# A hybrid encoder layer on one core: the raw sums of the FFN weights formed in the mixer, and seven products in every down projection

## The chip, the core and the metric

The kernel runs on one core of a Trainium2 chip. The time is what the device takes from the first to the last instruction of one execution and what lies around it, in microseconds (us); the figure given is the median of several runs. The engines: TensorE (PE; its weight loads are PEld in the profile), VectorE (DVE), ScalarE (ACT), GpSimd (POOL) and SyncE (SP), which here issues every DMA. Each engine runs its own instructions strictly in the order of the program and waits for others by semaphores.

## The reference, cut to what matters

2048 frames of a new stream and 64 frames of a running one (2112 tokens of 1024 features) pass through one layer in float32:

```
h = rmsnorm(x);  proj = h @ w_in
x = x + concat(gated_delta(proj), multiscale_pool(proj)) @ w_out
h = rmsnorm(x)
x = x + (silu(h @ w_gate) * (h @ w_up)) @ w_down      # 1024 -> 2816 -> 1024
y = rmsnorm(x)
```

The first addition is the mixer, the second the FFN. The change touches how the weights `w_gate`, `w_up` and `w_down` are prepared, and how the product with `w_down` is formed for a third of the tokens.

## The kernel before, in words

A float32 number is held as two float32r parts, hi and lo (a copy rounded by ACT, and by DVE what is left); each product of two such numbers is three matmuls: hi*hi, hi*lo, lo*hi. Making the two parts is called a split below: one cast on ACT and one subtraction on DVE.

The mixer runs over four blocks of 512 tokens (the first with the 64 more). Each block projects 21 column tiles (`pp`), runs the chunked delta rule of four heads (an inverse by doubling: the masked factors `Um` come from POOL, the products `py` and `pt` from PE, then `TV` from DVE; `NOUT` and `NX` say how many such chunks may be ahead of the one in use), pools, and projects out (`pz`) to `x2d` in DRAM.

The FFN runs over three blocks of 704 tokens. `gate_up` handles one of the 22 tiles f of 128 hidden features. It forms gate and up for both halves of the tokens (352 each) with seven products for the eight quarter products (Strassen's scheme): the weight factors are the quarters 11, 12, 22 and the sums S1 to S4 of quarters, the token factors 11, 21, 22 and T1 to T4. A product is 12 matmuls of 352 columns into one of the PSUM tiles x, y, z (`px`, `py`, `pz` in the profile); x is read by DVE twice on the way (tiles g and u) before the last product goes on into it.

The weights for this come from `prep_strassen`. The first time, in FFN block 0, it loads four raw quarters of a tile f, forms S1 to S4 on POOL (tiles `wrS`), splits all seven factors (`ws`, `wsS`) and stores the split S1 to S4 to DRAM (`gsd`). In blocks 1 and 2 it loads those four back in split form and splits only 11, 12 and 22.

The down projection runs over groups of 4, 4, 2, 4, 4, 4 tiles f. In block 0 it is dense: `down` takes eight column tiles m and both token halves, three matmuls for each f (PSUM tile d), adds into `y` on DVE, with the hidden features split by gate_up itself into `h3t`. In blocks 1 and 2 (`SDOWN`) it uses seven products: `factors` forms from each pair of tiles f the seven token factors (`hq` and `h7`; four sums on POOL, seven splits), `prep_down` forms for each pair of column tiles the raw sums on POOL (`wrda`, `wrdb`) from two loaded tiles (`wrdt`, `wrdl`) and splits seven factors (`wsd`, `wsdS`), and `down_strassen` adds the products dx, dy, dz into `y` in seven additions. The last group of block 2 is dense in both.

The order on every engine is set by `Machine`: it records all instructions, gives each a cost and a rank (its place in the program, moved by boosts for urgent ones), and lists them engine by engine as a list scheduler does. A `Chain` is a generator whose steps are mixed into the main program as its clock of PE work goes on; a step's rank comes from where it is mixed in, but the scheduler may place an instruction earlier when its engine is free and its operands are there.

The lines that the change meets:

```
SDOWN = (1, 2)
NY, NLEV, NOUT, NX = 3, 3, 5, 3
```

Of the kernel before, what the change touches and what calls it, by code (L numbers as in the profile page):

```python
# [11 lines left out]
F32 = mybir.dt.float32  # L12
F32R = mybir.dt.float32r
AF = mybir.ActivationFunctionType
ALU = mybir.AluOpType
# [3 lines left out]
P = 128  # L19
# [27 lines left out]

SDOWN = (1, 2)
# [305 lines left out]
def hybrid_kernel(ctx, tc, a, o):  # L354
# [88 lines left out]
    gsd = {nm: dpool.tile([NF, P, 1024], F32, tag=f"g{nm}", name=f"g{nm}") for nm in KEEP}  # L443
    hpd = dpool.tile([NB2, 7, 4, P, N2], F32, tag="hpd", name="hpd")
# [50 lines left out]
    def halves(b, gi):  # L495

        return ((0,), (1,)) if (b, gi) == (NB2 - 1, len(groups) - 1) else ((0, 1),)

    def plain(b, gi):
        return b not in SDOWN or len(halves(b, gi)) > 1  # L500

# [71 lines left out]
    def prep_strassen(key):  # L573
# [33 lines left out]
    def prep_down(m, f0, G):  # L607
# [654 lines left out]

    def new_o(B, pool=None, tag="op", bufs=2):
        four = [(pool or opool).tile([P, 4, 2, MB], F32R, tag=tag or f"h{k}", name=f"op{k}_{B.j}", bufs=bufs) for k in range(2)]
        B.o, B.o4 = [four[k // 4][:, k % 4] for k in range(KT)], four[0]
# [70 lines left out]
    for j in range(NBLK):  # L1336
# [13 lines left out]
        for h in range(NH):  # L1350
# [126 lines left out]
    def gate_up(b, f):  # L1477
# [44 lines left out]
        return raw if b in SDOWN else h3t[f % 6]  # L1522
# [54 lines left out]
    six = [opool.tile([P, 3, 2, TB2], F32R, tag="op", name=f"h3_{i}", bufs=2) for i in range(2)]  # L1577
    h3t = [six[i // 3][:, i % 3] for i in range(6)]
# [10 lines left out]
    for op in order:  # L1589
        b = op[1]  # L1590
        if op[0] == "gu":
# [6 lines left out]
            if b in SDOWN:  # L1598
                gi = max(g for g, (f0, G) in enumerate(groups) if f0 <= f)
                if plain(b, gi):  # L1600
                    if f == groups[gi][0] or f == groups[gi][0] + 2:
                        two = opool.tile([P, 2, 2, TB2], F32R, tag="op", name=f"h3l{f}", bufs=2)
                    for i in range(2):
                        split(two[:, f % 2], slice(i * N2, (i + 1) * N2), h3[f][:, i])
                    h3[f] = two[:, f % 2]
                elif f % 2:
                    h3[f] = factors(b, f, h3.pop(f - 1), h3[f])
# [29 lines left out]
NY, NLEV, NOUT, NX = 3, 3, 5, 3  # L1637
# [16 lines left out]
WAIT_STAT = 8.46  # L1654

# [110 lines left out]
```

## Time and profile before

| | us |
|---|---|
| median of 3 runs | 2418.33 (2416.62 to 2418.92) |
| span of the profiled execution | 2413.8 |
| PE busy | 2363.0 (98%) |
| DVE busy | 1744.6 (72%) |
| ACT busy | 1276.2 (53%) |
| POOL busy | 970.7 (40%) |
| DMA | 471.39 MB, mean 195 GB/s |

The profile is of one execution, whose span is given; the page states no separate time for that execution, so its own time is its span and the few us that lie around it. A row of a group gives the count, the busy time of the group, the mean duration of one instruction, and the idle time before them with what ended it. PE's matmuls overlap, so the mean of one (322 ns for 352 columns) is more than its share of the time; busy time over count is the share. In rows by stage, each stage begins with its limits and length, then the busy time of each engine with its instructions in brackets; the last three figures are PE's granted clock, the busy share of the DMA engines and GB/s. With a tile's name the same rows count that tile's instructions alone, and engines without any are left out.

### The profile page before, as it was taken

The page shows a single profiled execution, that of the slowest core. Times are in us where ns is not written, and L with a number is a line of the kernel's source. Part 1 is how long each engine was busy: PE and PEld are TensorE (multiplying, and loading weights), DVE is VectorE, ACT ScalarE, POOL GpSimd, SP SyncE. Part 2 cuts the span into 40 slices and gives each one's busy share as a digit, 9 for nine tenths or more (in the row PEclk, how much of TensorE's full clock was granted, in tenths as well). Part 3 has the DMA queues.
Part 4 walks back from the last instruction along what each step waited for, and adds up shares of the span by engine and source line. Part 5 has one row for each costly group of instructions (what it writes and reads, how often), then busy time and mean ns, then how long its engine had stood idle before and what let it go on. Part 6 is the DMA issues. An engine that isn't in the chain of part 4 may idle for free.

```text
span 2413.8 us, 42035 instructions
## 1 busy us (share of the span) xinstructions
PE 2363.0 (98%) x14811; PEld 2190.4 (91%) x14811; DVE 1744.6 (72%) x3065; ACT 1276.2 (53%) x2849; POOL 970.7 (40%) x1130
## 2 busy tenths in 40 slices
PE   8999999999999999999999999999999999999998
PEld 7889798778787878899999999999999999999998
DVE  7998774675467786787676765778777778777676
ACT  6665654563456464573454555554444564545444
POOL 1646442454246752365232235454222564223121
PEclk9999999999999999999999999999999999999999
DMA  7644566355555564987554557766644586454653
GB/s 266 222 156 151 174 221 217 134 181 175 179 182 182 186 196 138 317 298 238 200 183 166 184 199 237 238 227 204 224 157 147 163 292 216 144 168 166 202 171 109
DMA packets 219107, 471.39 MB, mean 195 GB/s; under 512 B 27408, under 2 KB 85776, under 8 KB 218896
## 3 DMA queue, kind: packets, MB, share of 16 engines
q1 hardware_dynamic: 218896, 468.71, 57.9%
q8 instruction: 116, 1.90, 0.3%
q14 instruction: 95, 0.78, 0.1%
HBM read 354.81 MB, written 113.80 MB: 194 GB/s over the span
## 4 chain that ended last, share of the span: by engine, by line
PE 80%; DVE 10%; DMA 4%; ACT 3%; issue 3%; POOL 1%; SPq 0%; DVEq 0%; POOLq 0%; ACTq 0%
PE pp L278 16%; PE px L278 16%; PE pz L278 11%; PE d L278 8%; PE py L278 7%; PE dx L278 5%; PE dy L278 3%; PE pk_p L278 2%; DVE hq L278 2%; PE pt_p L278 2%; PE dz L278 1%; ACT hr L278 1%; DVE hr L278 1%; PE px_p L278 1%; PE gr_p L278 1%
## 5 line engine op out<-in xcount | busy, mean ns | idle before, releaser
L278 PE MATMUL pp<-h,wsp 128*128 128x512 f32 (+1 forms) x2480 | 560.0, 367 | 3.9 <-DVE wsp L278 2.6
L278 PEld LDWEIGHTS pp<-h,wsp 128*128 128x128 f32 x2480 | 402.4, 191 | 53.7 <-ACT wsp L278 3.4
L278 POOL TENSOR_TENSOR Um_p<-Gst_p,lmask 128x256 f16<-128x256 f32 x224 | 169.9, 772 | 121.1 <-PE py_p L278 97.1
L278 PE MATMUL pz<-op,wsp 128*128 128x512 f32 (+1 forms) x960 | 215.7, 366 | 2.9 <-ACT op L278 2.6
L278 ACT CAST ws<-wr 128x512 fp32r<-128x512 f32 x198 | 121.9, 617 | 177.3 <-PE dx L278 46.9
L278 DVE TENSOR_TENSOR ws<-wr,ws 128x512 fp32r<-128x512 f32 x198 | 164.6, 835 | 45.9 <-ACT ws L278 40.9
L278 PEld LDWEIGHTS pz<-op,wsp 128*128 128x128 f32 x960 | 155.8, 190 | 23.0 <-ACT op L278 3.2
L278 PE MATMUL d<-h,wsd 128*128 128x352 f32 x1056 | 169.6, 322 | 0.5 <-ACT h L278 0.5
L278 PEld LDWEIGHTS d<-h,wsd 128*128 128x128 f32 x1056 | 168.5, 188 | 0.8 <-ACT h L278 0.8
L278 DVE TENSOR_TENSOR TV_p<-TV_p,pt_p 128x512 f16<-128x512 f16 x192 | 129.2, 681 | 43.1 <-PE pt_p L278 38.6
L278 PE MATMUL px<-hBT,ws 128*128 128x352 f32 x792 | 141.3, 326 | 12.7 <-DVE u L278 12.5
L278 POOL TENSOR_TENSOR wrS<-wr,wrS 128x512 f32<-128x512 f32 x44 | 63.9, 1452 | 209.2 <-DMA wrS<-in_wu_dram 97.3
L278 ACT ACTIVATE hr<-g 128x352 f32<-128x352 f32 x132 | 65.7, 498 | 153.7 <-DVE g L278 152.7
L278 PEld LDWEIGHTS px<-hBT,ws 128*128 128x128 f32 x792 | 127.9, 188 | 19.3 <-DVE u L278 18.5
L278 PE MATMUL px<-hA,ws 128*128 128x352 f32 x792 | 141.9, 322 | 0.1
L278 PE MATMUL px<-hA,wsS 128*128 128x352 f32 x792 | 138.6, 323 | 3.3 <-ACT g L278 3.2
L278 PE MATMUL pz<-hB,ws 128*128 128x352 f32 x792 | 141.5, 322 | 0.0
L278 PE MATMUL py<-hB,wsS 128*128 128x352 f32 x792 | 140.4, 322 | 0.0
L278 PE MATMUL px<-hBT,wsS 128*128 128x352 f32 x792 | 137.8, 322 | 1.3 <-ACT g L278 1.3
L278 PE MATMUL py<-hA,wsS 128*128 128x352 f32 x792 | 138.5, 323 | 0.1
L278 POOL TENSOR_TENSOR q<-hr,hr 128x352 f32<-128x352 f32 x40 | 45.0, 1126 | 231.5 <-DVE hr L278 230.1
L278 PEld LDWEIGHTS px<-hA,wsS 128*128 128x128 f32 x792 | 128.4, 188 | 5.4 <-ACT g L278 5.2
(613 smaller groups left out, 5737.4 us busy)
## 6 DMA issues: line engine op xcount, KB each, us to landing
wsS<-gS SPq DMA_DIRECT2D x176, 512.0 KB, 4.5
wsp<-wnd SPq DMA_DIRECT2D x126, 512.0 KB, 3.3
gS<-wsS SPq DMA_DIRECT2D x88, 512.0 KB, 4.4
wr<-in_wg_dram SPq DMA_DIRECT2D x132, 256.0 KB, 3.0
wnd<-wsp SPq DMA_DIRECT2D x42, 512.0 KB, 5.0
xd<-x2d SPq DMA_DIRECT2D x96, 176.0 KB, 3.2
wr<-in_wu_dram SPq DMA_DIRECT2D x66, 256.0 KB, 3.6
wrd<-in_wd_dram SPq DMA_DIRECT2D x56, 256.0 KB, 3.5
```

The source lines that it names most:

```text
L278: getattr(getattr(self.nc, op.eng), name)(*args, **kw)
```

## The change

A chain `weight_sums` is added and started when the first head of the mixer's second block is taken up. For each of the 22 tiles f it loads the four raw quarters, forms S1 to S4 on POOL in place (tiles gs0 to gs3, one buffer each) and stores them unsplit to DRAM (`grd`, named rS1 to rS4 in the rows). Then, for each group and each pair of column tiles of `w_down`, it loads two tiles, forms the four sums in place (ds0, ds1) and stores them to `drd`.

`prep_strassen` in FFN block 0 loads all seven raw factors, four of them from `grd`, and forms none. `prep_down` loads its two tiles of sums from `drd`. `SDOWN` goes: block 0 uses `factors`, `prep_down` and `down_strassen` as the others do, and `h3t` with the splits in gate_up goes. `NOUT` falls from 5 to 3 and `NX` from 3 to 2, which frees the space for the four buffers.

```diff
-SDOWN = (1, 2)
...
+    grd = {nm: dpool.tile([NF, P, 512], F32, tag=f"r{nm}", name=f"r{nm}") for nm in KEEP}
+    drd = dpool.tile([KT // 2, len(FGROUPS), 2, P, 512], F32, tag="drd", name="drd")
...
     def plain(b, gi):
-        return b not in SDOWN or len(halves(b, gi)) > 1
+        return len(halves(b, gi)) > 1
...
-        for nm, src in (("11", "11"), ("S1", "21"), ("22", "22"), ("12", "12")):
-            get(nm, src)
-        for nm in ("S3", "S2", "S4"):
-            raw[nm] = wtiles(nm, True)[0]()
-        gt = nc.gpsimd.tensor_tensor
-        gt(out=raw["S3"], in0=raw["11"], in1=raw["S1"], op=ALU.subtract)
-        gt(out=raw["S1"], in0=raw["S1"], in1=raw["22"], op=ALU.add)
-        gt(out=raw["S2"], in0=raw["S1"], in1=raw["11"], op=ALU.subtract)
-        gt(out=raw["S4"], in0=raw["12"], in1=raw["S2"], op=ALU.subtract)
+        for i, nm in enumerate(FW):
+            raw[nm] = wtiles(nm, i % 2 == 1)[0]()
+            nc.sync.dma_start(out=raw[nm], in_=grd[nm][key[1]] if nm in grd else q[nm])
...
-        gt = nc.gpsimd.tensor_tensor
-        left, right = slice(0, n), slice(n, 2 * n)
-        gt(out=s31[:, left], in0=top[:, left], in1=low[:, left], op=ALU.subtract)
-        gt(out=s31[:, right], in0=low[:, left], in1=low[:, right], op=ALU.add)
-        gt(out=s24[:, left], in0=s31[:, right], in1=top[:, left], op=ALU.subtract)
-        gt(out=s24[:, right], in0=top[:, right], in1=s24[:, left], op=ALU.subtract)
+        gi = [f for f, _ in groups].index(f0)
+        for i, x in enumerate((s31, s24)):
+            nc.sync.dma_start(out=x[:, : 2 * n], in_=drd[m, gi, i, :, : 2 * n])
+        right = slice(n, 2 * n)
...
+    def weight_sums():
+        gt = nc.gpsimd.tensor_tensor
+        new = lambda i, nm: gp.tile([P, 512], F32, tag=f"s{i}", name=nm, bufs=1)
+        for f in range(NF):
+            q = [new(i, f"gs{i}_{f}") for i in range(4)]
+            a11, a21, a22, a12 = q
+            for t, (nm, i) in zip(q, (("wg", 0), ("wu", 0), ("wu", 1), ("wg", 1))):
+                nc.sync.dma_start(out=t, in_=a[nm][f][:, i * 512 : (i + 1) * 512])
+            yield LAT_SUM
+            gt(out=a22, in0=a21, in1=a22, op=ALU.add)
+            gt(out=a21, in0=a11, in1=a21, op=ALU.subtract)
+            yield LAT_SUM
+            gt(out=a11, in0=a22, in1=a11, op=ALU.subtract)
+            gt(out=a12, in0=a12, in1=a11, op=ALU.subtract)
+            for nm, t in (("S1", a22), ("S3", a21), ("S2", a11), ("S4", a12)):
+                nc.sync.dma_start(out=grd[nm][f], in_=t)
+            yield LAT_SUM
+        at = 0
+        for gi, (f0, G) in enumerate(groups):
+            n = G // 2 * P
+            left, right = slice(0, n), slice(n, 2 * n)
+            for m in range(KT // 2):
+                top, low = (new(at + i, f"ds{i}_{gi}_{m}") for i in range(2))
+                at = 2 - at
+                for t, mm_ in ((top, m), (low, m + KT // 2)):
+                    nc.sync.dma_start(out=t[:, : 2 * n], in_=a["wd"][mm_][:, f0 * P : (f0 + G) * P])
+                yield LAT_SUM / 2
+                gt(out=low[:, right], in0=low[:, left], in1=low[:, right], op=ALU.add)
...
+                for i, t in enumerate((low, top)):
+                    nc.sync.dma_start(out=drd[m, gi, i, :, : 2 * n], in_=t[:, : 2 * n])
+                yield LAT_SUM / 2
...
+            if h == 0 and j == 1:
+                Chain(weight_sums())
...
-            if b not in SDOWN:
-                split(h3t[f % 6], slice(i * N2, (i + 1) * N2), e)
...
-NY, NLEV, NOUT, NX = 3, 3, 5, 3
+NY, NLEV, NOUT, NX = 3, 3, 3, 2
...
+LAT_SUM = 4.5
```

Three places in the order of the instructions. First POOL in the first block of the mixer, ahead of its first inverse (chist, ext and EL are small copies); before:

```order
L278 COPY chist_145<-ext0_4_170 128x3
L278 COPY ext0_9_232<-chist_145 128x3
L278 COPY ext0_9_232<-consts_93 128x3
L278 COPY chist_145<-ext0_8_177 128x3
L278 COPY EL_p0_0_0_215<-TV32_p0_0_0_213 128x2
```

and now:

```order
L276 TENSOR_TENSOR gs2_0_917<-gs1_0_916,gs2_0_917 128x512
L276 TENSOR_TENSOR gs1_0_916<-gs0_0_915,gs1_0_916 128x512
L276 COPY chist_150<-ext0_8_182 128x3
L276 COPY ext0_9_237<-chist_150 128x3
L276 COPY ext0_9_237<-consts_98 128x3
L276 TENSOR_TENSOR gs0_0_915<-gs2_0_917,gs0_0_915 128x512
L276 TENSOR_TENSOR gs3_0_918<-gs3_0_918,gs0_0_915 128x512
L276 COPY EL_p0_0_0_220<-TV32_p0_0_0_218 128x2
```

The sums of the first tile f stand in POOL's order from its row 25 on, a block earlier than the chain is started in the program; the last sum is its row 662 of 1099, shortly before the inverses of the fourth block. The sums of nine tiles f are ahead of the end of the second block's first inverse.

Next POOL in the second block of the mixer, within the inverse of head 1 (Um3 to Um6 are its masked factors); before:

```order
L278 TENSOR_TENSOR Um3_p1_1_0_1122<-Gst_p1_1_0_1045,lmask_140 128x256
L278 COPY EL_p1_1_1_1091<-TV32_p1_1_1_1089 128x2
L278 TENSOR_TENSOR Um4_p1_1_0_1137<-Gst_p1_1_0_1045,lmask_140 128x256
L278 TENSOR_TENSOR Gst_p1_1_1_1095<-Gam_p1_1_1_1094,consts_93 128x256
L278 TENSOR_TENSOR Um0_p1_1_1_1129<-Gst_p1_1_1_1095,lmask_140 128x256
```

and now:

```order
L276 TENSOR_TENSOR Um3_p1_1_0_1139<-Gst_p1_1_0_1062,lmask_145 128x256
L276 COPY ext1_3_1321<-chist_150 128x3
L276 TENSOR_TENSOR gs2_10_1363<-gs1_10_1362,gs2_10_1363 128x512
L276 TENSOR_TENSOR Um4_p1_1_0_1155<-Gst_p1_1_0_1062,lmask_145 128x256
L276 TENSOR_TENSOR gs1_10_1362<-gs0_10_1361,gs1_10_1362 128x512
L276 TENSOR_TENSOR Um5_p1_1_0_1170<-Gst_p1_1_0_1062,lmask_145 128x256
L276 TENSOR_TENSOR gs0_10_1361<-gs2_10_1363,gs0_10_1361 128x512
L276 TENSOR_TENSOR gs3_10_1364<-gs3_10_1364,gs0_10_1361 128x512
```

A sum now stands between any two Um of this inverse, and an Um behind it can start only when it is done.

Last SP, where the raw weights of FFN block 0's fourth tile f (number 120 in the names) are loaded; before:

```order
L278 DMA wr11_120_3034<-in_wg_dram 128x512
L278 DMA wrS1_120_3035<-in_wu_dram 128x512
L278 DMA y3_0_3115<-x2d_81 128x704
L278 DMA gS1_86<-wsS1_119_3028 128x1024
L278 DMA wr22_120_3036<-in_wu_dram 128x512
```

and now:

```order
L276 DMA wrS1_120_3176<-rS1_90 128x512
L276 DMA gS3_88<-wsS3_118_3158 128x1024
L276 DMA wr12_120_3178<-in_wg_dram 128x512
L276 DMA gS1_86<-wsS1_119_3169 128x1024
L276 DMA wr11_120_3175<-in_wg_dram 128x512
L276 DMA wrS4_120_3180<-rS4_93 128x512
L276 DMA wrS2_120_3177<-rS2_91 128x512
L276 DMA gS4_89<-wsS4_119_3173 128x1024
L276 DMA wrS3_120_3179<-rS3_92 128x512
```

Seven raw loads a tile f stand where four stood, between the same stores of split sums. SP's order has 1449 DMAs before and 1923 now.

More of the change, by code (lines that the diff above doesn't have):

```diff
@@ L1261, in fold_pool @@
                 yield LAT_APPLY
+    def weight_sums():
[26 more added lines that the diff above has]
+                gt(out=low[:, right], in0=low[:, left], in1=low[:, right], op=ALU.add)
+                gt(out=low[:, left], in0=top[:, left], in1=low[:, left], op=ALU.subtract)
+                gt(out=top[:, left], in0=low[:, right], in1=top[:, left], op=ALU.subtract)
+                gt(out=top[:, right], in0=top[:, right], in1=top[:, left], op=ALU.subtract)
+                for i, t in enumerate((low, top)):
+                    nc.sync.dma_start(out=drd[m, gi, i, :, : 2 * n], in_=t[:, : 2 * n])
+                yield LAT_SUM / 2
     def new_o(B, pool=None, tag="op", bufs=2):
@@ L1521, in gate_up @@
         finish(0, g1, x)
-        return raw if b in SDOWN else h3t[f % 6]
+        return raw
     def down(b, gi, h3, ys, which, done):
@@ L1576, in hybrid_kernel @@
     fpos = {2: (0, 1), 4: (0, 2, 1, 3)}
-    six = [opool.tile([P, 3, 2, TB2], F32R, tag="op", name=f"h3_{i}", bufs=2) for i in range(2)]
-    h3t = [six[i // 3][:, i % 3] for i in range(6)]
     h3, ys = {}, {}
@@ L1597, in hybrid_kernel @@
             h3[f] = gate_up(b, f)
[L1598 to L1607, printed above, removed]
+            gi = max(g for g, (f0, G) in enumerate(groups) if f0 <= f)
+            if plain(b, gi):
+                if f == groups[gi][0] or f == groups[gi][0] + 2:
+                    two = opool.tile([P, 2, 2, TB2], F32R, tag="op", name=f"h3l{f}", bufs=2)
+                for i in range(2):
+                    split(two[:, f % 2], slice(i * N2, (i + 1) * N2), h3[f][:, i])
+                h3[f] = two[:, f % 2]
+            elif f % 2:
+                h3[f] = factors(b, f, h3.pop(f - 1), h3[f])
             if f == NF - 1 and b + 1 < NB2:
```

## The prediction

> **What bounds the kernel now.** I read the page first, then the time by stage, then the waits in the two kinds of FFN block, last the instructions behind one wait. From the page: the span, the busy times and the chain that ended last.
>
> ```profile
> span 2413.8 us, 42035 instructions
> PE 2363.0 (98%) x14811; PEld 2190.4 (91%) x14811; DVE 1744.6 (72%) x3065; ACT 1276.2 (53%) x2849; POOL 970.7 (40%) x1130
> PE 80%; DVE 10%; DMA 4%; ACT 3%; issue 3%; POOL 1%; SPq 0%; DVEq 0%; POOLq 0%; ACTq 0%
> ```
>
> TensorE (PE) is the bound, so only removed matmuls or removed waits of PE can gain. The stages are cut by first and last start of a tile's matmuls (us, after the three durations): gate_up begins at 1003.2, block 0's dense down projection ends at 1474.3; the mixer I cut at 250, 480 and 700, block 1 at 1939.
>
> ```profile
> L278 PE MATMUL px<-hA,ws x792: 317/322/430, 1003.2 to 2359.6; 128*128 128x352 f32 x198
> ```
>
> ```profile
> L278 PE MATMUL d<-h,wsd x1056: 317/322/428, 1090.1 to 1474.1; 128*128 128x352 f32 x176
> ```
>
> ```profile
> core 0: us, PE busy (x) PEld busy (x) DVE busy (x) ACT busy (x) POOL busy (x), PEclk, DMA share, GB/s
> 0.00:250.00 250.00, 235.09 (x1785) 214.59 (x1786) 211.18 (x459) 159.19 (x399) 113.16 (x177) 0.99 0.60 202
> 250.00:480.00 230.00, 229.82 (x1529) 196.66 (x1529) 154.14 (x292) 124.45 (x310) 94.37 (x140) 1.00 0.54 182
> 480.00:700.00 220.00, 219.44 (x1302) 178.41 (x1301) 135.46 (x250) 110.51 (x278) 93.01 (x138) 1.00 0.51 173
> ...
> 1003.20:1474.30 471.10, 466.79 (x2910) 464.64 (x2909) 336.21 (x509) 241.64 (x488) 184.99 (x142) 1.00 0.63 219
> 1474.30:1939.00 464.70, 454.88 (x2783) 445.21 (x2783) 349.24 (x593) 238.57 (x494) 191.89 (x200) 1.00 0.60 199
> 1939.00:2366.00 427.00, 419.76 (x2575) 412.01 (x2574) 302.16 (x523) 212.66 (x440) 132.11 (x143) 1.00 0.58 191
> ```
>
> The clock is granted in full, so it plays no part. What one matmul of 352 columns costs comes from the dense down projection of block 0, by the tile wsd (columns PE, PEld, DVE, ACT; the first row is block 0, the second block 1).
>
> ```profile
> 1003.20:1474.30 471.10, 169.44 (x1056) 168.49 (x1056) 35.88 (x48) 27.79 (x48) 1.00 0.63 219
> 1474.30:1939.00 464.70, 76.62 (x391) 64.40 (x390) 37.10 (x48) 22.91 (x48) 1.00 0.60 199
> ```
>
> 169.44/1056 = 0.1605 us. By it block 0's 2910 matmuls need 467.1 us of its 471.1: 4.0 us are lost. Block 1's 2783 need 446.7 of 464.7: 18.0 are lost. Block 2 loses 427.0 - 2575 x 0.1605 = 13.7. This is the main reading: where seven products already run, about two thirds of what they save is waited away again (block 1 is only 6.4 us shorter than block 0). The waits of PE in block 0 (first row) and block 1 name the place.
>
> ```profile
> PE px L278 <- DVE u L278: 1.0, 2, 0.8
> ```
>
> ```profile
> PE px L278 <- DVE u L278: 6.5, 7, 1.5
> ```
>
> The last product of gate_up goes on into a PSUM bank that VectorE (DVE) must first read (tile u). The longest of these waits, at 1628.44:
>
> ```profile
> 1626.73 1.22 DVE L278 TENSOR_TENSOR wsdS<-wrda,wsdS 128x512 fp32r<-128x512 f32 x1
> 1627.87 0.51 DVE L278 TENSOR_TENSOR u<-px,u 128x352 f32<-128x352 f32 x1
> ```
>
> ```profile
> 1626.39 1.01 POOL L278 TENSOR_TENSOR wrda<-wrdt,wrdl 128x256 f32<-128x256 f32 x1
> 1627.36 1.17 POOL L278 TENSOR_TENSOR wrdb<-wrdt,wrdb 128x256 f32<-128x256 f32 x1
> ```
>
> ```profile
> 1628.44 1.87 PE L278 MATMUL px<-hBT,ws 128*128 128x352 f32 x10 [1.50 <-DVE u L278]
> ```
>
> A split of a weight took 1.22 us on DVE while GpSimd (POOL) formed the raw sums of the down weights, and u stood behind it. The undisturbed duration of such splits is their median (min/median/max ns, block 0):
>
> ```profile
> L278 DVE TENSOR_TENSOR ws<-wr,ws x66: 676/692/1781, 1004.0 to 1456.0; 128x512 fp32r<-128x512 f32 x66
> L278 DVE TENSOR_TENSOR h<-hr,h x44: 509/519/1619, 1019.9 to 1447.6; 128x352 fp32r<-128x352 f32 x44
> ```
>
> **The change, part by part.** First its price list, in block 0: the splits of h (tile h, columns PE, PEld, DVE, ACT), the adds into y (tile y, DVE, ACT) and the sums wrS (DVE, ACT, POOL); then, in block 1, what block 0 will get: the factors' splits (tile hq; a further 11 under h, the second row), their sums (tile hr, whose last column is POOL), and the splits wsdS.
>
> ```profile
> 1003.20:1474.30 471.10, 169.44 (x1056) 168.49 (x1056) 37.53 (x44) 21.13 (x44) 1.00 0.63 219
> 1474.30:1939.00 464.70, 13.71 (x43) 7.92 (x42) 6.68 (x11) 0.00 (x0) 1.00 0.60 199
> ```
>
> ```profile
> 1003.20:1474.30 471.10, 48.54 (x95) 0.50 (x1) 1.00 0.63 219
> ```
>
> ```profile
> 1003.20:1474.30 471.10, 72.81 (x85) 51.48 (x84) 122.38 (x84) 1.00 0.63 219
> ```
>
> ```profile
> 1474.30:1939.00 464.70, 155.52 (x876) 142.07 (x876) 59.51 (x77) 36.79 (x77) 1.00 0.60 199
> ```
>
> ```profile
> 1474.30:1939.00 464.70, 82.16 (x132) 90.80 (x176) 50.71 (x44) 1.00 0.60 199
> ```
>
> ```profile
> 1474.30:1939.00 464.70, 100.43 (x528) 86.48 (x528) 37.57 (x48) 27.74 (x48) 1.00 0.60 199
> ```
>
> *PE work.* Block 0's down projection goes from 8 tiles x 2 halves x 22 x 3 = 1056 matmuls to 4 x 7 x 11 x 3 = 924: 132 x 0.1605 = **-21.2 us**, all of it on the bound. The matmuls of blocks 1 and 2 stay.
>
> *Block 0 loses its slack.* DVE there: 336.2 - 37.5 (h) + 59.5 + 6.7 (factors) - 35.9 (wsd) + 37.1 + 37.6 (wsd and wsdS in seven-product form) + 72 more adds x 0.511 = 36.8 (4 x 7 x 6 = 168 for 96) gives 440.5 us. POOL falls from 185.0 by 122.4 (wrS) and gains 50.7, to 113.3. What POOL stretches on DVE here is at least 37.5 - 44 x 0.519 = 14.7 (h) and 72.8 - 85 x 0.692 = 14.0 (splits of the sums), 28.7 us for 185.0 of POOL; with the other two-input instructions I estimate 0.25 us for each us of POOL, so 72 less of it gives 18 back: 422 us. In a block of some 460 that is 92%, where it was 71% and block 1 has 75%. The split of every weight stays in block 0 (four more a tile f than in block 1: 88 x 0.692 = 61 us), and it lies ahead of u on DVE. ScalarE, at 241.6 us, takes the added casts (some 40 us) without becoming late. From below the loss of PE stays at 4.0 us (0); from above block 0 gives back more than its saving (+30). Nearest is block 1's 18.0: its collisions with the sums go, fuller DVE comes. I take a loss of 16: **+12**.
>
> *Blocks 1 and 2 without sums.* The removed groups (two of four, x36 each):
>
> ```profile
> L278 POOL TENSOR_TENSOR wrda<-wrdl 128x256 f32<-128x256 f32 x36 | 32.5, 904 | 0.0
> L278 POOL TENSOR_TENSOR wrdb<-wrda,wrdt 128x256 f32<-128x256 f32 x36 | 30.0, 832 | 10.4 <-DVE wsdS L278 8.9
> ```
>
> Some 0.87 us each, 144 of them, 125 us of POOL, leave the stretches where u is late. Of 18.0 + 13.7 lost, block 0's 4.0 a block is the best to hope for (-23.7); 0 if other work stands ahead of u instead. The factors' sums still collide, so I take **-9**. The two loads that replace four sums for each tile are late only if the queue is (below).
>
> *The sums in the mixer.* 88 sums of 512 columns and 96 of at most 256 are added; the first are wrS now:
>
> ```profile
> L278 POOL TENSOR_TENSOR wrS<-wrS,wr 128x512 f32<-128x512 f32 x44 | 64.3, 1461 | 32.7 <-DVE hr L278 14.9 <-DMA wr<-in_wu_dram 10.7 <-DVE wsS L278 3.5
> ```
>
> 88 x 1.46 + 96 x 0.87 = 212 us of POOL. The order puts them between POOL's first 30 and 660 rows, not in blocks 1 and 2 alone: nine tiles f are summed before the second block's inverses are done. So in 700 us POOL goes from 300.5 to 513, and DVE, by the 0.25, from 500.8 to 554; in the first 250 us DVE goes from 211 by about 12 to 223 (89%), and there PE already loses 15 us, start included. After 250 us PE idles 0.7 us in 450 and DVE has a third free: hidden, as long as no sum holds up an Um (the masked factors of the inverse) behind it on POOL. The shorter look-ahead (NOUT 3, NX 2) starts the inverses later in the order; that I cost at nothing, since projections still stand between their steps. From below 0, from above the +30 of the second rival; half of the first 250 us' 12, and 2 later: **+8**.
>
> The Trainium skill (SBUF — State Buffer, "SBUF: two separate sides") says that a DVE instruction with two SBUF inputs and one of GpSimd exclude each other for a whole instruction. By that rule alone each moved us of POOL that meets such an instruction costs a whole us of DVE, a rival below; the maxima above (1781 against 692) agree with the lock, and the 0.25 says how seldom it strikes.
>
> *Transfers.* Each tile f of block 0 reads three raw tiles more (66 x 0.262 = 17.3 MB), its down weights 96 loads for 48 (+11.5 MB). That is 103.2 MB (471.1 x 219) to 132 MB, 284 GB/s. The ceiling shows at the block's start:
>
> ```profile
> 975.00:1003.20 28.20, 28.20 (x126) 23.34 (x126) 20.00 (x35) 14.30 (x28) 5.78 (x5) 1.00 0.95 314
> 1003.20:1025.00 21.80, 21.80 (x138) 21.80 (x137) 16.39 (x23) 13.07 (x26) 11.65 (x8) 1.00 0.99 356
> ```
>
> On average there is room (284 of 356), at the start none: the first tiles' raw sums now stand on the SP queue among the last stores of x2d. Ends 0 and +12 (4 MB at 0.33 MB/us); the weights come a tile ahead, so **+2**. SP, which issues all of this in order, gets 474 more issues (1923 for 1449 in its order) at the median of such a row:
>
> ```profile
> L278 SPq DMA_DIRECT2D xd<-x2d x96: 319/374/985, 712.0 to 1688.7; - x96
> ```
>
> 719 us of 2414 are no bound, but a store of a sum that waits for POOL holds back the loads behind it, mixer weights among them; that is in the +8.
>
> The sum is -21.2 + 12 - 9 + 8 + 2 = -8.2 us. The profiled span would be 2405.6; the median of the runs lies 4.5 us above that span (2418.33), so 2410 us.
>
> **Rivals.** *The whole gain*: the mixer hides the sums, block 0 loses no more than 8 us, blocks 1 and 2 give 14: -21.2 + 4 - 14 + 0 = -31, 2387 us. For it: PE's idle time of 0.7 us between 250 and 700. Against it: block 1's 18.0.
> *GpSimd holds the mixer (slower)*: a sum waits for its loads or, its buffers being single, for the last tile's stores, and the Um behind it waits too, then PE. There are 46 such chunks; at 0.65 us of PE each this is 30, 2432 us. It decides from (8.2 + 8)/46 = 0.35 us a chunk. For it: POOL runs strictly in order and becomes 73% busy; against it: the order leaves several Um ahead of each sum.
> *DVE bounds block 0 (slower)*: at 92%, each collision lands on PE; +28 for +12 gives 2426 us. *Transfers bound its start*: +12 for +2, 2420. *DVE bounds the mixer (slower)*: if each us of a sum stretched DVE by a us, DVE would have 500.8 + 212 = 713 us in 700, at least 13 us more than there are; with as much again for the turns between engines +26 for +8 gives 2428 us. For it: DVE is 84% busy in the first 250 us. Against it: 0.25 in FFN block 0. (By the Trainium skill, SBUF — State Buffer, "Who interferes with whom", full overlap would do this.)
> *The change does not do what it says*: sums lie in block 0 of the mixer, the part where DVE is fullest; this is in the +8.
>
> **How the numbers follow.** Forecast (2403 to 2417) 0.40, of which 0.10 lies within 0.2% (4.8 us, about what a measurement can tell from no change); the whole gain 0.18; POOL holds the mixer 0.17; DVE bounds the mixer 0.05; DVE bounds block 0 0.13; transfers 0.07, of which most is no change. Faster 0.30 + 0.18 + 0.02 from milder forms of the others = 0.50, same 0.10 + 0.05 = 0.15, slower 0.35. The range goes from inside the whole gain (2390) to the second rival's 2432 and a little more, 2436.
>
> **What would show it.** Right: 924 matmuls of the down projection in block 0, which lasts about 462 us; PE waiting for u there as often as in block 1 now; DVE near 90% in it; fewer waits for u in blocks 1 and 2; the mixer ending 8 us later, mostly lost in the first 250 us. Wrong: PE waiting for Um or py in the mixer with POOL's sums ahead of them waiting for DMA; block 0 as long as before; raw sums landing late at its start.

## The result, and the profile after

| | before | after |
|---|---|---|
| median, us | 2417.51 (20 runs, 2414.49 to 2421.03) | 2422.69 (20 runs, 2419.01 to 2428.88) |
| span of the profiled execution, us | 2413.8 | 2421.8 |
| ratio, with its 95% interval | | 1.0024 (1.0018 to 1.0030) |

The change costs a quarter of a per cent, where 0.3% less was forecast. The page of the changed kernel: span, busy times, the chain that ended last.

```profile
span 2421.8 us, 42846 instructions
PE 2354.6 (97%) x14679; PEld 2168.4 (90%) x14679; DVE 1825.8 (75%) x3218; ACT 1310.9 (54%) x2930; POOL 967.0 (40%) x1094
PE 74%; DVE 11%; DMA 7%; ACT 3%; issue 3%; POOL 1%; SPq 0%; DVEq 0%; POOLq 0%; ACTq 0%
```

PE has the 132 matmuls less, but its busy time falls by 8.4 us only, where 132 x 0.1605 are 21.2, and it idles 67.2 us where it idled 50.8. The two profiled executions lie 8.0 us apart, the medians 5.2; the stages below are those of the profiles. The end of the mixer is the last start of a `pz`, first in the kernel before, then in the changed one.

```profile
L278 PE MATMUL pz<-op,wsp x960: 288/389/796, 309.3 to 1002.9; 128*128 128x512 f32 x115, 128*128 128x288 f32 x77
```

```profile
L276 PE MATMUL pz<-op,wsp x960: 288/389/791, 318.7 to 1036.6; 128*128 128x512 f32 x115, 128*128 128x288 f32 x77
```

The 33.7 us between them contain 24 matmuls of gate_up that now run ahead of the last `pz` (24 x 0.1605 = 3.9). Block 0's down projection ends at 1491.4, block 1's at 1955.3; before, at 1474.1 and 1941.4. So by stage, in us:

| stage | before | after | difference | forecast |
|---|---|---|---|---|
| mixer | 1002.9 | 1032.8 | +29.9 | +8 |
| FFN block 0 | 471.2 | 458.6 | -12.6 | -21.2 + 12 + 2 = -7.2 |
| FFN block 1 | 467.3 | 463.9 | -3.4 | -9 with block 2 |
| FFN block 2, end | 472.4 | 466.5 | -5.9 | |

The FFN gained 22 us, the mixer gave back 30. The mixer's figure is good to some 3 us: in three kernels below whose mixer is the one of before, it ends 2.8 to 3.7 us later than here. The stretches of the changed kernel (columns as in the prediction: PE, PEld, DVE, ACT, POOL busy, clock, share of the DMA engines, GB/s), three of the mixer and then the FFN's blocks:

```profile
0.00:250.00 250.00, 232.47 (x1744) 209.76 (x1745) 221.94 (x442) 153.93 (x389) 156.53 (x202) 0.99 0.82 260
250.00:480.00 230.00, 224.55 (x1471) 190.62 (x1471) 165.65 (x286) 119.86 (x301) 145.92 (x170) 0.99 0.83 266
480.00:700.00 220.00, 211.41 (x1224) 166.75 (x1223) 153.85 (x241) 107.10 (x262) 162.50 (x206) 0.99 0.85 273
1036.60:1491.40 454.80, 448.87 (x2771) 443.75 (x2770) 385.07 (x668) 278.49 (x567) 103.65 (x92) 1.00 0.81 276
1491.40:1955.30 463.90, 455.24 (x2781) 446.43 (x2780) 338.11 (x594) 242.99 (x507) 130.91 (x119) 1.00 0.72 234
1955.30:2374.00 418.70, 414.81 (x2564) 410.64 (x2563) 286.45 (x521) 210.94 (x436) 64.83 (x59) 1.00 0.67 213
```

Against the rows of before, POOL grows in all three mixer stretches (300.5 to 465 us), DVE by 40 us in 700, and the DMA engines' share from some 0.55 to 0.83. PE idles 14.0 us in the two stretches from 250 to 700, where it idled 0.7; by 700 it has started some 177 matmuls fewer (4439 for 4616). No single wait of PE is large; the longest of 250 to 1003:

```profile
PE pz L276 <- ACT op L276: 5.3, 3, 3.5
PE pc L276 <- DVE Rt L276: 5.3, 5, 1.9
PE pz L276 <- DMA wsp<-wod: 3.2, 2, 2.2
PE ptk_p L276 <- DVE Yqk L276: 1.8, 2, 1.0
PE pp L276 <- DMA wsp<-wnd: 1.7, 2, 1.1
PE pk_p L276 <- DVE Sp L276: 1.2, 1, 1.2
PE py_p L276 <- POOL Um_p L276: 0.5, 1, 0.5
```

`Um`, the wait that the prediction named, holds PE directly for 0.5 us only. But a wait can cost PE more than its length. Behind the longest of these, for `op`, stand:

```profile
1001.45 4.39 PE L276 MATMUL pz<-op,wsp 128*128 128x512 f32 x11 [3.52 <-ACT op L276]
1006.08 10.72 PE L276 MATMUL pz<-op,wsp 128*128 128x512 f32 x46 [0.24 <-DVE wsp L276]
```

Eleven matmuls take 0.40 us each, the next 46 take 0.23: from 1001.5 to 1004.9 the granted clock is 0.51. The changed kernel's mixer has four stretches at half clock, 17.1 us together, each right behind waits of PE; 10.2 us of them lie between 250 and 700. Before there were three, 10.2 us together, none of them between 250 and 700. By estimate (half of 10.2) the clock costs 5 us there, beside the idle time. Over its 20 runs the changed kernel was granted a clock of 0.994 in the mean, the kernel before 0.996 in the runs beside the experiments.

SP, between 250 and 720, waits for the stores of the sums to land before the same buffers can be loaded again:

```profile
SPq L276 <- DMA drd<-ds: 50.5, 29, 4.3
SPq L276 <- DMA rS<-gs: 46.8, 28, 4.3
```

and POOL, up to 700, stands in front of sums whose loads have not landed:

```profile
POOL ds L276 <- DMA ds<-in_wd_dram: 33.2, 16, 4.0
...
POOL gs L276 <- DMA gs<-in_wg_dram: 16.9, 6, 8.1
...
POOL gs L276 <- DMA gs<-in_wu_dram: 12.7, 3, 8.4
```

So four suspects for the mixer's 30 us: GpSimd's sums (through VectorE, or through GpSimd's own order), the traffic, SP's queue, and the shorter look-ahead.

### The profile page after: what moved, and what is told of

Read it like the earlier page. It is cut to its first block, busy times and chain, and to the rows that moved or that the text cites. A ratio compares the mean times of both kernels' runs of the same rounds, so it can differ in the third digit from the quotient of the medians.

```text
span 2421.8 us, 42846 instructions
## 1 busy us (share of the span) xinstructions
PE 2354.6 (97%) x14679; PEld 2168.4 (90%) x14679; DVE 1825.8 (75%) x3218; ACT 1310.9 (54%) x2930; POOL 967.0 (40%) x1094
## 4 chain that ended last, share of the span: by engine, by line
PE 74%; DVE 11%; DMA 7%; ACT 3%; issue 3%; POOL 1%; SPq 0%; DVEq 0%; POOLq 0%; ACTq 0%
PE px L276 17%; PE pp L276 13%; PE pz L276 11%; PE dx L276 8%; PE py L276 8%; PE dy L276 4%; PE dz L276 2%; DVE y L276 2%; PE pk_p L276 2%; PE pt_p L276 1%; PE d L276 1%; DVE hq L276 1%; PE py_p L276 1%; DVE Yqk L276 1%; DMA rS<-gs 1%
## 5 line engine op out<-in xcount | busy, mean ns | idle before, releaser
L276 POOL TENSOR_TENSOR q<-hr,hr 128x352 f32<-128x352 f32 x62 | 68.9, 1111 | 806.2 <-DVE hr L276 742.2
L276 POOL TENSOR_TENSOR Um_p<-Gst_p,lmask 128x256 f16<-128x256 f32 x224 | 175.9, 798 | 69.4 <-PE py_p L276 50.9
L276 PEld LDWEIGHTS pz<-op,wsp 128*128 128x128 f32 x960 | 155.7, 190 | 30.1 <-ACT op L276 6.3
L276 DVE TENSOR_TENSOR y<-y,dx 128x352 f32<-128x352 f32 x272 | 136.8, 517 | 49.3 <-PE dx L276 47.7
L276 PE MATMUL dx<-hq,wsd 128*128 128x352 f32 x620 | 153.2, 325 | 2.9 <-DVE y L276 1.4
L276 PE MATMUL dy<-hq,wsdS 128*128 128x352 f32 x744 | 149.2, 323 | 1.5 <-DVE y L276 1.5
L276 PE MATMUL dx<-hq,wsdS 128*128 128x352 f32 x744 | 145.5, 325 | 2.9 <-DVE y L276 2.2
L276 POOL TENSOR_TENSOR gs<-gs,gs 128x512 f32<-128x512 f32 x88 | 125.9, 1430 | 36.9 <-DMA gs<-in_wg_dram 16.9
```

The costliest lines, as they stand in the source:

```text
L276: getattr(getattr(self.nc, op.eng), name)(*args, **kw)
```

## The experiments

Each run gives a ratio to the kernel before, run on the same chip beside it. To compare runs of different chips, ratios are turned into us by 2417.5. "Mixer late" is the last start of `pz` in the profiled execution against 1002.9; in most runs with the short look-ahead it contains the 24 matmuls of gate_up (3.9 us) that run ahead.

### Without the chain: the look-ahead

```diff
-                Chain(weight_sums())
...
-            nc.sync.dma_start(out=raw[nm], in_=grd[nm][key[1]] if nm in grd else q[nm])
+            nc.sync.dma_start(out=raw[nm], in_=q[FROM.get(nm, nm)])
...
-            nc.sync.dma_start(out=x[:, : 2 * n], in_=drd[m, gi, i, :, : 2 * n])
+            nc.sync.dma_start(out=x[:, : 2 * n], in_=a["wd"][m + KT // 2 * i][:, f0 * P : (f0 + G) * P])
```

Left out: all sums of weights, their loads and stores in the mixer; the FFN loads raw quarters in their place.

> Left out: the mixer's chain of sums altogether (its loads, its GpSimd sums and its stores); the FFN loads raw quarters in the place of the sums, as many bytes as before, so its products are of unsummed weights. NOUT 3 and NX 2 stay. If the sums are what costs the mixer its 30 us (its last pz matmul at 1036.6 us in the changed kernel, 1002.9 before), it ends within 4 us of 1003 and the time falls to about 2392 us. If the shorter look-ahead costs it, the mixer still ends near 1030 and the time stays near 2418.

Measured: 0.9886 (0.9871 to 0.9901), 27.6 us faster than before; the mixer ends at 1004.3, 1.4 us late, or 2.5 us early without the 24 matmuls of gate_up. The shorter look-ahead costs nothing that shows. And this is what the change is worth if its sums were free: the 33.4 us between it and the changed kernel are the sums and what belongs to them.

### Transfers alone, and sums alone

In the first run the chain keeps its loads and stores and loses its sums (`gt(...)` lines removed; the FFN works with weights that were not summed). In the second it keeps the sums, on four zeroed tiles, and loses loads and stores (`dma_start` lines of the chain removed, FFN as in the run above).

> Left out: the GpSimd sums alone; the loads into the four single buffers and the stores from them stay, so the FFN gets unsummed weights. If SyncE's queue and the transfers are the cause (SyncE waits 97 us between 250 and 720 us for the landing of a store before it reloads its buffer, and holds weight loads back), most of the 30 us stays: mixer end 1025 or later, time about 2413 or more. If GpSimd's sums on the port shared with VectorE are the cause, the mixer ends near 1008 and the time is about 2396.

> Left out: the loads and stores of the sums; the GpSimd sums are made, in the same steps, on four tiles of zeros, and the FFN loads raw quarters in their place. If GpSimd's sums (a longer VectorE, an Um held up behind a sum) are the cause, the mixer ends at 1025 or later and the time is 2413 or more; if the queue and the transfers are, it ends before 1010 and the time is about 2396. If the two share the 30 us, both this and the run with transfers alone lie near 1018.

Transfers alone: 0.9921 (0.9905 to 0.9936), 8.5 us above the run without the chain. Sums alone: 1.0138 (1.0123 to 1.0154), 61 us above it, twice the whole. The second run doesn't decompose the change, because with no loads to wait for, the scheduler drew the sums to the start. The first 250 us without the chain, and with sums alone:

```profile
0.00:250.00 250.00, 236.22 (x1808) 218.14 (x1808) 213.63 (x461) 159.11 (x402) 116.91 (x180) 0.99 0.60 197
```

```profile
0.00:250.00 250.00, 209.40 (x1448) 187.05 (x1449) 235.15 (x370) 134.66 (x335) 209.95 (x221) 0.95 0.53 175
```

POOL takes 93 us more there, DVE 21.5 us more while finishing 91 instructions fewer, and PE idles 27 us more, with a granted clock of 0.95. What it does show is that the place of a sum matters.

### The sums at one place, with and without transfers

To hold the place fixed, a dependence that only the scheduler sees was put on each step of the chain, so that nothing of it is ordered ahead of the matmuls that stand before it, and a chunk of down sums is due every 10 us.

```diff
+        if self.hold is not None:
+            op.preds[id(self.hold)] = self.hold
...
+            machine.hold = next(p for p in reversed(machine.ops) if p.eng == "tensor")
...
-                yield LAT_SUM / 2
+                yield 10.0 / 2
```

> The changed kernel with its sums spread: a step of the chain is ordered no earlier than the matmuls that stand ahead of it when it is taken, and a chunk of the down sums is due every 10 us, where it was 4.5; they lie from some 250 us on to the mixer's end, none in the first part, where VectorE is fullest. Same work and same traffic. Theory 1 (what the mixer loses is GpSimd's sums beside a full VectorE and bunched in two stretches): the mixer ends 10 to 18 us late in place of 30, time 2404 to 2412 us. Rival (the loss is the traffic, or SP's queue held by the stores of sums, whatever the place): mixer 25 to 35 us late, time 2416 to 2426.

> The same placement without any transfer for the sums: GpSimd adds four zeroed tiles in place of the weights and nothing is stored, the FFN loads raw quarters where it would load sums, so the output is not the reference's. Theory 1: the sums alone cost most, mixer 8 to 15 us late, time 2398 to 2406 against 2390.6 without the chain. Rival (traffic): at most 4 us late, time 2390 to 2395.

The complete kernel with sums spread: 1.0010 (1.0001 to 1.0019), 30.0 us above the run without the chain (the changed kernel: 33.4). Its mixer is 35.9 us late in the profile (by the same count the changed kernel's is 33.7), not 10 to 18: spreading the work moved the loss to later stretches and took little of it away. Theory 1 falls as it stood there; the mixer and the time (2418.9 us) are about what its rival had. The same sums at the same places without transfers: 0.9948 (0.9934 to 0.9962), 15.0 us above. With 8.5 for the transfers that makes 23.5 of 30; the difference is of the size of the intervals (3.5 us each), and the 8.5 was measured with the transfers where the changed kernel has them, not spread. So, roughly: half the loss is the sums, a quarter to a third the transfers, and the rest, if it is any, what they do to each other.

### Which way a sum costs PE

The prediction's working had sums cost PE through DVE, by 0.25 us for each us of POOL. The groups of DVE from 250 to 700, before and after (mean ns of one behind the busy time), show which instructions that is:

```profile
L278 DVE TENSOR_TENSOR TV_p<-TV_p,pt_p 128x512 f16<-128x512 f16 x76 | 51.5, 683 | 24.7 <-PE pt_p L278 23.2 <-issue 1.1
L278 DVE SCALAR_TENSOR_TENSOR Yqk<-ext,consts,Yqk 128x512 f32<-128x512 f32 x48 | 37.8, 789 | 10.7 <-ACT Yqk L278 9.7
L278 DVE SCALAR_TENSOR_TENSOR Yvz<-ext,consts,Yvz 128x512 f32<-128x512 f32 x24 | 18.0, 751 | 6.6 <-ACT Yvz L278 6.1
```

```profile
L276 DVE TENSOR_TENSOR TV_p<-TV_p,pt_p 128x512 f16<-128x512 f16 x70 | 46.8, 682 | 22.1 <-PE pt_p L276 20.5 <-POOL ext L276 0.7 <-POOL osq_s L276 0.6
L276 DVE SCALAR_TENSOR_TENSOR Yqk<-ext,consts,Yqk 128x512 f32<-128x512 f32 x48 | 44.5, 927 | 7.6 <-ACT Yqk L276 6.9
L276 DVE SCALAR_TENSOR_TENSOR Yvz<-ext,consts,Yvz 128x512 f32<-128x512 f32 x24 | 24.0, 998 | 3.4 <-ACT Yvz L276 3.0
```

`TV`, with one of its inputs in PSUM (`pt_p`), keeps its 683 ns; `Yqk` and `Yvz`, with both tensor inputs in SBUF, grow by 138 and 247. The Trainium skill (SBUF — State Buffer, "SBUF: two separate sides") says that a DVE instruction with two SBUF inputs and a GpSimd instruction that reads SBUF exclude each other for a whole instruction; the rows agree on which are hit. The sums do it, not the traffic beside them: the means of `Yqk` and `Yvz` are 831 and 769 without the chain, 830 and 769 with transfers alone, and 1043 and 982 with the spread sums alone. To see whether this stretch sets the time, GpSimd was given copies in place of sums: two copies of one input for each sum of two. Left out as before: the sums themselves and their transfers.

```diff
-            gt(out=a22, in0=a21, in1=a22, op=ALU.add)
+            for _ in range(2):
+                gc(a22, a21)
...
```

> As the run with the sums spread over the mixer and no transfers (2404.0 us, 13.4 above the run without the chain, 2390.6), but GpSimd copies a zeroed tile twice for each sum: one input in place of two, about the same time on GpSimd. No sum is formed, and the FFN loads raw quarters where it would load sums, so the output is not the reference's. If the sums cost by what they stretch on VectorE, and copies do not stretch it (next to GpSimd's one-input instructions its two-input ones kept their length in the traces so far, in few cases): 2390 to 2396. If they cost because Um and the rest of GpSimd's own work wait their turn behind them: 2401 to 2407.

Measured: 0.9956 (0.9940 to 0.9973), 16.9 us above the run without the chain, where the sums made 15.0. From 250 to 700, with no chain, with sums, with copies:

```profile
250.00:700.00 450.00, 449.01 (x2808) 369.95 (x2809) 287.70 (x543) 236.98 (x585) 183.81 (x270) 1.00 0.55 179
```

```profile
250.00:700.00 450.00, 445.21 (x2754) 365.99 (x2753) 317.79 (x526) 230.37 (x576) 328.25 (x378) 1.00 0.54 177
```

```profile
250.00:700.00 450.00, 447.68 (x2806) 370.49 (x2805) 302.52 (x541) 235.00 (x585) 328.05 (x495) 1.00 0.55 177
```

POOL is as busy with copies as with sums (328 us), DVE's growth is halved (30.1 to 14.8 us; `Yqk` and `Yvz` take 884 and 864 ns, so copies do stretch them), and the time is the same within the intervals. So over the whole run the price does not follow the stretch of DVE: the same busy time of GpSimd costs as much with half of it. The rows above are less clear. In these 450 us, against the run without the chain, the sums cost PE 3.8 us of idle time and 54 matmuls, the copies 1.3 us and two; the rest of the copies' 17 us comes after 700. Where the sums stand, their stretch is not ruled out as the cause. The other candidate is GpSimd's own order: counted in the traces, no `Um` stands right behind a sum before the change, 41 do after, 36 in the run with the spread sums alone and 47 with copies. That this is the path was not shown: PE waits for `Um` itself for 2.1 us at most in these three, and no run moved `Um` ahead of the sums.

### Traffic, or SP's queue

The transfers with little to wait for: loads go to two tiles that nobody reads, stores read two others. SP's waits for transfers of the chain, up to 1005 us, fall from 63 us in the run with transfers alone to 21; what is left are loads that wait for an earlier load into the same tile. Left out: the sums, and the FFN's loads of them.

```diff
-            q = [new(i, f"gs{i}_{f}") for i in range(4)]
+        q = [gp.tile([P, 512], F32, tag=f"s{i}", name=f"s{i}", bufs=1) for i in range(2)]
+        z = [gp.tile([P, 512], F32, tag=f"s{i}", name=f"s{i}", bufs=1) for i in (2, 3)]
...
-                nc.sync.dma_start(out=grd[nm][f], in_=t)
+                nc.sync.dma_start(out=grd[nm][f], in_=z[j % 2])
```

> The loads and stores of the sums at their places in the order as in the changed kernel, same sizes, but none of them waits for another engine or for a transfer of this chunk: loads go into two tiles that nobody reads, stores read two other tiles that hold zeros. No sum is formed, and the FFN loads raw quarters where it would load sums, so the output is not the reference's. The run with waiting transfers and no sums stood at 2397.6 us, the one without both at 2390.6. If SP, held in order by stores that wait for their loads, is the cost: 2390 to 2393. If the traffic itself is the cost (share of the DMA engines above 0.8): 2396 to 2399.

Measured: 0.9929 (0.9916 to 0.9943), 10.4 us above the run without the chain, no better than the 8.5 with waiting transfers. So the transfers cost by being there, by their traffic or by their many issues on SP, and not by these waits. The DMA engines are busy 0.87 to 0.89 of the time up to 700, where the run without the chain has 0.54 to 0.60. Landing of the mixer's own weights in the first 320 us (KB each, median us), without the chain and here:

```profile
wrp<-in_win_dram SPq DMA_DIRECT2D x42, 256.0 KB, 3.6
wsp<-wnd SPq DMA_DIRECT2D x18, 512.0 KB, 3.6
```

```profile
wrp<-in_win_dram SPq DMA_DIRECT2D x42, 256.0 KB, 4.6
wsp<-wnd SPq DMA_DIRECT2D x18, 512.0 KB, 5.0
```

The changed kernel's own waits, 97 us behind stores of sums, are longer than those compared here, and no run took them away alone. That they cost nothing is likely, but not shown.

### One half of the sums moved, and none

Three complete kernels, each with seven products in all down projections: gate and up sums alone in the mixer; the same, held as above; down sums alone in the mixer, held. The other half is formed in the FFN as before. A fourth forms all of them in the FFN, with the look-ahead as before (`NOUT` 5, `NX` 3).

```diff
-            nc.sync.dma_start(out=x[:, : 2 * n], in_=drd[m, gi, i, :, : 2 * n])
+        gt(out=s31[:, left], in0=top[:, left], in1=low[:, left], op=ALU.subtract)
...
```

> Gate and up sums in the mixer as in the changed kernel, the down sums formed in the FFN as before the change. Theory 1 (a place with room on VectorE makes a sum cheap, the mixer's first 250 us do not): the mixer ends 9 to 13 us late, as the changed kernel was when its gate sums were done; block 0 about 472 us (20 us less than with all sums in the FFN), blocks 1 and 2 as before; time 2420 to 2428. Rival (traffic): the gate sums carry 46 of the 69 MB that the sums move in the mixer, so two thirds of the 30 us: mixer 18 to 22 late, time 2428 to 2436.

> Gate and up sums in the mixer, down sums formed in the FFN, as in the run that moved the gate sums alone (2426.8 us, mixer 25.6 us late), but a step is ordered no earlier than the matmuls ahead of it, so that no sum is drawn into the first 250 us. If the place where VectorE is fullest is what made the gate sums dear: mixer 10 to 16 us late, 2412 to 2418 us. If they cost by their number and traffic wherever they lie: 22 to 28 us late, 2423 to 2428.

> Down sums in the mixer, spread at 10 us a chunk from about 250 us on, the gate and up sums of block 0 formed in the FFN as before the change. Theory 1: mixer 6 to 10 us late, block 0 480 us, blocks 1 and 2 together 9 us less; time 2416 to 2426. Rival (down sums cost 20 us wherever they lie in the mixer): time 2430 to 2436.

> Complete. Seven products in all three blocks, with every raw sum formed where it is used, as before (block 0 on GpSimd too), NOUT 5 and NX 3. The mixer is that of before and ends at 1003. If block 0 gains by the fewer matmuls even with the sums beside it, as block 1 did before, it lasts 455 to 468 us (471.2 before, 458.7 changed) and the time is 2405 to 2415; if its sums (24 more column tiles of them, beside fuller VectorE) are what moving them was needed for, block 0 lasts 475 or more and the time is 2421 or more.

| sums in the mixer | ratio (95%) | against before, us | mixer late, us |
|---|---|---|---|
| none | 1.0069 (1.0052 to 1.0086) | +16.7 | 2.8 |
| down | 1.0031 (1.0019 to 1.0043) | +7.5 | 7.1 |
| gate and up | 1.0043 (1.0029 to 1.0057) | +10.4 | 25.6 |
| gate and up, held | 1.0017 (1.0007 to 1.0027) | +4.1 | 26.8, in the longest of its runs |
| both (the change) | 1.0024 (1.0018 to 1.0030) | +5.8 | 33.7 |

The first row is the main one: seven products in block 0 with the sums left where they were cost 16.7 us. Block 0 then looks like this:

```profile
1005.70:1497.00 491.30, 468.50 (x2792) 453.68 (x2792) 447.59 (x662) 271.32 (x558) 308.94 (x269) 0.98 0.59 203
```

DVE is 91% busy, and the block that took 471.2 us takes 491.3. Of this some 10 us are the clock, which was granted at half for 20.5 us of the block, each time behind waits of PE. So the two halves of the change must be judged apart: seven products in block 0 are a loss of 17 us, and moving the sums away earns 11 of it back. The gate sums' 25.6 us in the mixer (21.7 without the 3.9 of gate_up run ahead) are more than theory 1's 9 to 13 and fit the rival's 18 to 22, while the time, 2426.8 us, lies in theory 1's range; and they are two thirds of GpSimd's time for sums as well as of the traffic, so this doesn't make traffic the cause. The down sums' 7.1 are as theory 1 had it. Together that is 32.7, the change's 33.7. Holding the gate sums gave 6 us, a quarter of their price, between the two expectations; its profiled execution was the longest of nine (span 2429.9), so its stages are not compared.

### Sums due later after their loads

The edit, against the kernel with its sums spread:

```diff
-            yield LAT_SUM
+            yield 12.0
...
-                yield 10.0 / 2
+                yield 8.0
```

> The kernel with its sums spread (2418.9 us), but a sum is due 12 us (gate) or 8 us (down) after its loads, where it was 4.5 and 5; same work and traffic. GpSimd stood 31 us in ten waits for loads of the gate sums in that run. If it is these waits that make sums and transfers together dearer than each alone (28 us against 13.4 and 7): 2410 to 2414. If not: 2417 to 2421.

Measured: 1.0160 (1.0145 to 1.0175), 39 us slower than before. It doesn't answer the question. POOL's waits for loads stayed (28 us in six waits), and the last sums now stand beyond the mixer, at 1055 us. The mixer itself ended 20.0 us late, where it was 35.9 with the spread sums, and the FFN's start has one wait that is most of the loss:

```profile
PE py L279 <- ACT wsS L279: 35.1, 1, 35.1
```

In the 34 us from 1032.8 to 1066.8, within this wait and behind it, the granted clock is 0.50.

### The sums kept where they are formed

Two complete kernels on the basis of the kernel before: block 0 dense, gate sums formed in it, mixer untouched. In the first, block 1 stores the down sums that it forms and block 2 loads them. In the second, block 0 forms them from the raw tiles that its dense down projection holds anyway, and blocks 1 and 2 load them.

```diff
+    PAIRS = [m for i in range(KT // 2) for m in (i, i + KT // 2)]
...
+            if fresh and m >= 4:
+                down_sums(m - 4, gi, G // 2 * P, state["top"], raw)
...
-        gt(out=s31[:, left], in0=top[:, left], in1=low[:, left], op=ALU.subtract)
...
+            nc.sync.dma_start(out=x[:, : 2 * n], in_=drd[m, gi, i, :, : 2 * n])
...
-        for m in range(KT):
+        for m in PAIRS if b == 0 else range(KT):
```

> The kernel before, with one edit: block 1 keeps the raw down sums that it forms (48 stores), block 2 loads them in place of forming them. No sum is added anywhere and the mixer and block 0 stay as they were. If GpSimd's sums are what makes u late in the blocks with seven products: block 2 some 5 us shorter, 2411 to 2414 us. If other work stands ahead of u all the same: 2416 to 2418, as before.

> The kernel before, with the down sums formed once, in block 0 of the FFN, from the raw tiles that its dense down projection loads anyway (taken in pairs m, m + 4), kept and loaded in blocks 1 and 2: 96 sums move to a stretch where VectorE is 71% busy and PE loses 4 us, no load is added for them, block 0 stays dense. If room on VectorE makes a sum cheap: block 0 up by 0 to 4 us, blocks 1 and 2 down by 9 together, 2409 to 2414 us. If a sum costs PE some 0.1 us wherever it stands (30 us for 184 sums in the mixer): block 0 up by 9 to 15, 2417 to 2424.

Kept from block 1: 0.9980 (0.9971 to 0.9988), 4.8 us faster than before. Kept from block 0: 0.9964 (0.9952 to 0.9977), 8.7 us faster, 2408.8 us, the best complete kernel here. Its blocks 0 and 1:

```profile
1006.60:1478.00 471.40, 466.94 (x2909) 464.76 (x2908) 344.88 (x508) 241.72 (x486) 266.11 (x236) 1.00 0.70 241
1478.00:1941.50 463.50, 455.63 (x2798) 447.79 (x2797) 333.43 (x594) 241.08 (x501) 121.35 (x109) 1.00 0.71 229
```

Block 0 takes 81 us more of POOL (185.0 before) and lasts 471.4 us, as before (471.2): there these sums cost PE nothing that shows, without loads of their own and with DVE at 73%. Blocks 1 and 2 are 3.8 and 7.1 us shorter; the mixer, not touched by the edit, ended 3.7 us later in this execution.

## Why the prediction was wrong, point by point

- **The failing step is the sums in the mixer**: +8 taken, +29.9 measured, against ends of 0 and +30. The step said "after 250 us PE idles 0.7 us in 450 and DVE has a third free: hidden". That no engine is full there doesn't mean that work is hidden: PE idled 14.0 us in those 450 with POOL at 69% and DVE at 71%, and ran 10.2 us of them at half clock. The loss was expected mostly in the first 250 us; there PE idled 2.6 us more and started 41 matmuls fewer. The likely reason is that spare time was read per engine, where the inverses are a chain through PE, DVE, ACT and POOL; by which way the sums hold up this chain stays open.
- **Its terms**: the sums about 15 us, the transfers 8.5 to 10; some 6 us are assigned to neither. The prediction had the mixer's traffic in no term; it counted that of block 0, and of the mixer only the wait of a store on SP, which no run shows to cost anything.
- **"The clock is granted in full"** held for the FFN's rows of before. In the mixer PE's waits bring stretches at half clock, and the changed kernel has more of them.
- **The 0.25 us of DVE for each us of POOL** held (40 us of DVE for 165 of POOL in 700 us, though with 32 instructions of DVE fewer), but the price did not follow it: half the stretch gave the same time.
- **PE work, block 0 and its start**: -21.2 + 12 + 2 forecast, -12.6 measured, within 6 us. DVE came to 385 us, not 422; with 2771 x 0.1605 = 444.7 of 454.8, 10.1 us are lost, not 16, and PE waits for u for 3.3 us, half of block 1's 6.5 before. No wait of PE for a transfer shows in this block, at 276 GB/s.
- **Blocks 1 and 2**: -9 forecast, -9.3 measured, in part by luck. By the prediction's own count (length less 0.1605 us a matmul) block 1 loses 17.5 us where it lost 18.3, and block 2 7.2 where it lost 13.5; the rest is matmuls that fall into other stages. In block 1 the waits for u went from 6.5 to 0.5 us, but those for g and y from 1.6 to 7.3. The run that keeps the sums from block 0, whose blocks 1 and 2 form no sums either, gives 10.9.
- **The look-ahead at nothing**: right, no loss shows without the chain.
- **The rivals**: "GpSimd holds the mixer", with 0.17, had the mixer's figure (+30) and the sign; its mechanism is half right. POOL does stand before late loads (63 us up to 700), but PE hardly waits for `Um` directly, and only about half of the loss is GpSimd's. "The whole gain" is what the run without the chain shows, at 2390 us. DVE is 85% busy in block 0 and 71% from 250 to 700, so it bounds neither; in the first 250 us it is at 89%. The time, 2422.7, lies in the range.
- **What was never asked**: what seven products in block 0 cost with the sums in place. The prediction took block 1's loss as block 0's bound and so saw the move as an extra; it is what makes block 0's saving possible, and it costs the mixer more than the saving.

## What to carry to other kernels

An idle third of an engine need not cover work that stands in order ahead of a serial chain through that engine: price moved work by the chain's engines together, and put its traffic into the sum of the stage it is moved to. When a change has two halves, ask for each alone, since one may be a loss that the other only mends. Before work is moved to another stage, look whether the stage that already holds its inputs can keep the result: here that gave 8.7 us, where the move cost 5.8.

## What the runs showed of the hardware

- DVE's stretch beside GpSimd's sums hits instructions with two inputs in SBUF and spares `TV`, which reads PSUM: 789 to 927 and 751 to 998 ns against 683 and 682. Transfers alone do not stretch them (830 and 769 ns for 831 and 769).
- GpSimd copies 128x512 float32 in 0.70 us (176 of them, 122.3 us), half the 1.41 us of a sum of two inputs, and for the same busy time stretches DVE by half as much.
- The transfers, with the DMA engines' share near 0.87 up to 700 us in place of 0.54 to 0.60, cost 8.5 to 10.4 us, and the mixer's weights land 1.0 to 1.4 us later beside them. Whether SP waits 63 or 21 us for them made no difference.
- A wait of PE can cost more than its length: behind 3.52 us without work, 11 matmuls of 512 columns took 0.40 us each at a granted clock of 0.51, where the next took 0.23.
